# Re-ranking the preparation of mixed rows and tying late ScalarE operations to the newest cast

## The chip, the cores and the metric

The kernel runs on one core of a Trainium2 chip. The metric is device time in microseconds (us) of one execution; several executions give a median. A profile was taken of one further execution.

## The reference, cut to what matters

One layer of a streaming encoder is computed for 2048 new frames (the prompt) and 8 short streams of 16 frames (the sample), all of width 1024, in float32:

```python
h = rmsnorm(x, g_mix_pre)
y, new_k, new_v, new_conv = parallel_mixer(h, ...)   # banded attention | depthwise conv, then @ w_out
x = x + rmsnorm(y, g_mix_post)
h = rmsnorm(x, g_mem_pre)
x = x + rmsnorm(memory_attention(h, mk, mv, w_mq, w_mo), g_mem_post)   # 4 heads, 256 memory tokens
h = rmsnorm(x, g_ffn_pre)
f = (silu(h @ w_gate) * (h @ w_up)) @ w_down
x = x + rmsnorm(f, g_ffn_post)
```

The outputs are the rows x of both groups and the updated caches.

## The kernel before, in words

**Arithmetic.** Every float32 product is made of three matmuls of two rounded parts: a value is cast to its high part on ScalarE (`nc.scalar.copy`), the low part is the difference (VectorE or GpSimd), and `mm3` (lines 268 to 270) adds high x high, high x low and low x high; `mm3h` (line 276) does the same for two halves of 512 columns. So ahead of each group of matmuls stands one cast and one subtraction per operand. Large products are built from seven block products instead of eight, with sums and differences of blocks around them.

**Order.** The program is written in Python loops; a scheduler then places each instruction on its engine's queue by rank (the order of tracing, raised by `high_priority(offset=...)`) and by when it expects its inputs. `issue_after(ins)` makes everything traced inside it stand behind the instruction `ins`. An engine runs its queue strictly in order, so an operation that waits holds up whatever stands behind it. Work that may float is kept in Python generators, from which a loop takes one step at a time with `next`.

**Stages.** The trace has them in this order: memory and input projections, banded attention, the mixing of rows (`mixout`, about 842 to 1100 us), the cross stage (`phase_cross`, about 1100 to 1422), gate and up (`gate_up`, about 1422 to 2400), and down.

**mixout** takes 17 tiles of 128 rows, the sample's tile first. For each tile 48 matmuls (line 276) multiply the mixed rows by the resident weight. `ahead(i)` prepares the tile after the next: `by_column` (GpSimd, line 952) lays out softmax weights, `prep` (lines 995 to 1014) loads the convolution's half (line 998), spreads the weights by one matmul (line 1003), multiplies the attention half (VectorE, 1006), casts both halves (ScalarE, 1012) and takes their low parts (VectorE, 1013), and `weigh` (937 to 946) prepares softmax weights of a later tile. Behind a tile follow Squares (1061), a GpSimd reciprocal root (1062, 286, 287), the scaling (VectorE, 1065), the residual and a store. From the third tile on, a generator `fill` (`cross_sample`) is drawn on: the sample's whole cross attention, whose weights are loaded (1114), cast (ScalarE, 1108) and split (VectorE, 1109). Its steps stand behind the newest low part, `last_prep`.

**phase_cross** takes 16 steps, 8 for the scores and 8 for the output, of seven products each in PSUM banks a, b, a, b, c, d, c. While a step multiplies, the generator `aforms` transposes and splits the rows of the next step (PE 1258, ScalarE 1267, VectorE or GpSimd 1268, sums at 1274 to 1292). The evictions (1457 to 1476) collect the blocks in the rows `ya` and `yb`, of which four tiles exist. What remains of a step floats in `tails`: `softmax` (max 1309, exps 1312, store 1317), `rows_out` (Square 1326, gain 1327, root 286/287, residual 1334, store 1335, a second norm by 294 and 1341), `forms_out` (GpSimd subtractions and stores, 1353 to 1362), `natural` (the same forms for rows loaded again: load 1374, Square 1377, root 1379/1380, scaling 1382, then GpSimd), and `combine`. The function `between`, called after each product, takes one step of each tail, behind the newest eviction.

**gate_up** multiplies weight forms (`wforms`: loads 1539, GpSimd sums 1546 to 1549, casts 1551, low parts 1552) by row forms (`tform`: loads 1526, transposes 1529, casts 1531, low parts 1532) and applies silu (copy 1588, Tanh 1595 and 1613, VectorE 1591 to 1616). Two more `natural` generators are left in `todo`; one step of it is taken per weight tile in group 0 from f = 5 on, behind `done`, the last VectorE operation (1616).

Of the kernel before, what the change touches and what calls it, by code (L numbers as in the profile page):

```python
# [8 lines left out]
F32 = mybir.dt.float32  # L9
F32R = mybir.dt.float32r  # L10
BF16 = mybir.dt.bfloat16
AF = mybir.ActivationFunctionType
# [5 lines left out]
P = 128  # L18
# [118 lines left out]
class Build:  # L137
# [842 lines left out]
    def mixout(self, ctx):  # L980
        nc, A = self.nc, self.A
        sbF, sbR = self.sbF, self.sbR
        (ft, fr), ff = self.flex(ctx, (2048, F32), (2048, F32R)), self.fa
        pool = (Region().lay(sbF, 34.5, ("wf", 4, 3), ("gbc", 4, 1))
                .at("fq", 2, (sbF, [4, 6, 8, 10])).at("ct", 2, (ff, [2, 10])).lay(ff, 0, ("an", 2, 1)).at("po", 4, (ff, [5]), (sbF, [0])).at("spo", 4, (ff, [22]))
                .lay(ff, 12, ("junk", 2, 1), ("xt", 4, 2), ("sh", 8, 1), ("ss", 0.03125, 6), ("rstd", 0.03125, 6),
                     ("nmx", 0.03125, 1), ("sm", 0.03125, 1), ("ri", 0.03125, 1)).lay(ff, 26, ("sgain", 4, 1))
                .at("mh", 4, (sbR, [40, 88])).at("ml", 4, (sbR, [44, 92]))
                .lay(sbR, 96, ("sTh", 4, 1), ("sTl", 4, 1)).lay(ft, 0, ("sT", 8, 1))
                .at("kvh", 4, (sbR, [64, 80]), (fr, [0])).at("kvl", 4, (sbR, [104, 84]), (fr, [4])))  # L990
        ps_y = ps_p = ps_so = Region().lay(self.ps, 0, ("y", 2, 4), ("p", 2, 2), ("so", 4, 1))
        for _ in self.wo_load:
            pass
        ws, self.w = self.wo, pool
        gbc = self.gain(pool, "g_mix_post", "gbc")
        def prep(t):
            ct = self.t(pool, [P, 4, P], F32, "ct", 2)
            nc.sync.dma_start(ct[:, :, :].rearrange("p a b -> p (a b)"), self.cs[t])
            if t == S_TILE:
                att = self.attS[:, :, :]  # L1000
            else:
                pt = self.t(ps_p, [P, 512], F32, "p")
                nc.tensor.matmul(pt[:, :], self.spread[:, :, :].rearrange("p o d -> p (o d)"),
                                 self.rj[:, :, :].rearrange("p j q -> p (j q)"), start=True, stop=True)
                an = self.t(pool, [P, 4, P], F32, "an", 1)
                nc.vector.tensor_tensor(an[:, :, :], self.attT[:, t, :, :],
                                        pt[:, :].rearrange("p (j q) -> p j q", q=P), ALU.mult)
                att = an[:, :, :]
            mh = self.t(pool, [P, KC, P], F32R, "mh", 2)
            ml = self.t(pool, [P, KC, P], F32R, "ml", 2)  # L1010
            for sl, src in ((slice(4, 8), ct[:, :, :]), (slice(0, 4), att)):
                nc.scalar.copy(mh[:, sl, :], src)
                self.last_prep = nc.vector.tensor_tensor(ml[:, sl, :], src, mh[:, sl, :].bitcast(F32), ALU.subtract)
            ready[t] = (mh, ml)

        def ahead(i):

            if 0 < i < len(order) - 1:
                self.by_column(order[i + 1])
                yield  # L1020
                prep(order[i + 1])
            yield
            if 0 < i < len(order) - 2:
                yield from self.weigh(order[i + 2], ps_p, "p")

        order = [S_TILE] + list(range(NPT))
        ready = {}
        with self.tc.high_priority(offset=HP2):
            for t in order[:2]:
                prep(t)  # L1030
        fill, due, self.last_tile = iter(()), 0.0, False
        for i, t in enumerate(order):
            mh, ml = ready.pop(t)
            self.last_tile = i >= len(order) - 2
            pre = ahead(i)
            xt = self.t(pool, [P, D], F32, "xt", 2)
            nc.sync.dma_start(xt[:, :], self.rows("x", t))
            if i in range(8, 16, 2):
                sums = self.combine(pool, 0, i // 2 - 4, 1)
            y = [self.t(ps_y, [P, 512], F32, "y")[:, :] for _ in range(2)]  # L1040
            for k in range(KC):
                if i >= 8 and k % 3 == 1:
                    next(sums, None)
                event = self.mm3h(y, mh[:, k, :], ml[:, k, :], ws[k][0], ws[k][1], k == 0, k == KC - 1)
                if k == 1:
                    self.mixed = event
                if k % 2:
                    next(pre, None)
                    due += RATE if i >= FROM else 0.0
                    while due >= 1:  # L1050
                        with self.tc.issue_after(self.last_prep.ins):
                            next(fill, None)
                        due -= 1
            for _ in pre:
                pass
            ss = self.t(pool, [P, 2], F32, "ss")
            junk = self.t(pool, [P, D], BF16, "junk")
            po = self.t(pool, [P, D], F32, "po")
            cols = [slice(o * 512, (o + 1) * 512) for o in range(2)]
            for o in range(2):  # L1060
                nc.scalar.activation(junk[:, cols[o]], y[o], AF.Square, accum_out=ss[:, o:o + 1])
            nc.gpsimd.tensor_tensor(ss[:, 0:1], ss[:, 0:1], ss[:, 1:2], ALU.add)
            r = self.rstd(pool, ss[:, 0:1], 1.0 / D)
            for o in range(2):
                nc.vector.scalar_tensor_tensor(po[:, cols[o]], y[o], r[:, :], gbc[:, cols[o]], ALU.mult, ALU.mult)
            nc.gpsimd.tensor_tensor(po[:, :], po[:, :], xt[:, :], ALU.add)
            nc.gpsimd.dma_start(self.x1[t], po[:, :])
            if i == 0:
                fill, due = self.cross_sample(pool, ps_so, ps_p), 0.0
        self.last_tile = True  # L1070
        for _ in fill:
            pass
# [129 lines left out]
    def phase_cross(self, ctx):  # L1202
# [48 lines left out]
        def aforms(src, out):  # L1251
# [12 lines left out]
            def split(x, engine):  # L1264
                hi = self.t(pool, [P, 4, P], F32R, "ah")
                lo = self.t(pool, [P, 4, P], F32R, "al")
                nc.scalar.copy(hi[:, :, :], x)
                engine.tensor_tensor(lo[:, :, :], x, hi[:, :, :].bitcast(F32), ALU.subtract)  # L1268
                out.append((hi, lo))

            p21, p22 = turn(xb, 0), turn(xb, 1)
# [94 lines left out]
        def natural(g, p):  # L1366
# [2 lines left out]
            xb = self.t(pool, [P, 2, 512], F32, "nb")[:n]  # L1369
            tt = self.t(pool, [P, 2, 512], F32, "nt")[:n]  # L1370
            dst = self.hn[g]
            for x, (t, r0) in zip((xa, xb), PAIRS[g][p][:2]):
                x2 = x.rearrange("p a b -> p (a b)")
                nc.sync.dma_start(x2, self.x2[t][r0:r0 + n, :])
                junk = self.t(pool, [P, D], BF16, "junk", 1)
                ss = self.t(pool, [P, 1], F32, "ss", 6)
                nc.scalar.activation(junk[:n, :], x2, AF.Square, accum_out=ss[:n, :])
                r = self.t(pool, [P, 1], F32, "rstd", 6)
                nc.gpsimd.tensor_scalar(r[:n, :], ss[:n, :], 1.0 / D, EPS, ALU.mult, ALU.add)
                nc.gpsimd.tensor_tensor(r[:n, :], r[:n, :], self.mhalf[:n, 0:1], ALU.pow)  # L1380
                yield
                nc.vector.scalar_tensor_tensor(x2, x2, r[:n, :], gffn[:n, :], ALU.mult, ALU.mult)
                yield
            nc.gpsimd.tensor_tensor(tt[:, 0, :], xb[:, 0, :], xa[:, 0, :], ALU.subtract)
            nc.gpsimd.dma_start(dst[:n, p, 0:2, :], xa)
# [27 lines left out]
        for s in range(2 * n):  # L1413
# [15 lines left out]
            def between(j):  # L1429
                if j >= 0 and s == n - 1:  # L1430
                    nbf.append(bform(f2, j))
                next(gen, None)
                if j == 2 and s + 2 <= last:
                    src[s + 2] = fetch(s + 2)
                if j == 1 and s == 2:
                    tails.append(natural(2, 2))
                if j == 4 and s in (1, 4):
                    tails.append(self.combine(pool, 1, s // 4 * 2, 2))
                for g in list(tails):
                    with self.tc.issue_after(self.evict.ins) if self.evict else ExitStack():  # L1440
                        over = next(g, tails) is not None
                    if over:
                        tails.remove(g)
# [58 lines left out]
    def gate_up(self, ctx):  # L1502
# [63 lines left out]
        for g in range(3):  # L1566
            n = sum(p[2] for p in PAIRS[g])
            for fp in range(NF // 2):
# [4 lines left out]
                for x in range(2):  # L1573
# [36 lines left out]
                    after(6)  # L1610
                    tt(x2, x2, c, ALU.add)
                    th = self.t(pool, [P, 3 * P], F32, "th")[:, :n]
                    nc.scalar.activation(th, x2, AF.Tanh, scale=0.5)
                    stt(th, th, 1.0, x2, ALU.add, ALU.mult)
                    dst = af[:, 3 if x == 0 else 5, :n]
                    done = stt(dst, th, 0.5, x3, ALU.mult, ALU.mult)
# [2 lines left out]
                    if f < NF - 1 or g < 2:  # L1619
                        w = wforms((f + 1) % NF)  # L1620
                    if g == 0 and f > 4:
                        with self.tc.issue_after(done.ins):
                            next(self.todo, None)
                    if turn:
                        for _ in self.todo:
# [241 lines left out]
```

## Time and profile before

| what | value |
|---|---|
| median of 3 runs | 2872.99 us (2871.47 to 2875.62) |
| the profiled execution's own time | 2869.33 us |
| its span | 2867.6 us |
| TensorE busy | 2818.1 us, 98% of the span |
| VectorE, GpSimd, ScalarE busy | 75%, 52%, 49% |
| mean granted TensorE clock | 0.998 |

The profile's names: PE is TensorE's matmul, PEld its weight load, DVE VectorE, ACT ScalarE, POOL GpSimd, SP the queue that issues most DMAs. L1012 is line 1012 of the kernel before. A group of rows such as "x2" is that many instructions in a row. The bracket at a row's end is the engine's idle time before it and what ended that. `psb` names PSUM, `sbf`, `sbr`, `sbx` and `flexb` name regions of SBUF.

### The profile page before, as it was taken

Reading aid. Unit: us, or ns where it says so; the run is one execution under the profiler, and the core shown is the slowest. Engines: PE = TensorE matmul, PEld = TensorE weight load, DVE = VectorE, ACT = ScalarE, POOL = GpSimd, SP = SyncE. Lnnn points to the kernel's source line nnn. Section 1 sums busy time; section 2 is a strip of 40 time slices with the busy share of each in tenths; the row PEclk is TensorE's granted clock in tenths of the full one; section 3 lists DMA queues with packets and bytes.
Section 4 is the critical chain, followed back from the end, with each engine's and each line's share of the span. In section 5 each row is a group of like instructions: output and inputs, shape, how many; then the busy total and the mean of one; then the engine's idle time right before and its main releaser. Section 6 shows DMA issues by size and latency. Waiting matters only on the chain.

```text
span 2867.6 us, 44831 instructions
## 1 busy us (share of the span) xinstructions
PE 2818.1 (98%) x16056; PEld 2549.2 (89%) x16056; DVE 2154.6 (75%) x3172; ACT 1394.7 (49%) x2803; POOL 1492.2 (52%) x1342
## 2 busy tenths in 40 slices
PE   9999999999999999999999999999999999999998
PEld 8999999988887767888789999999999998888786
DVE  6696795889885337678788888887879997555756
ACT  5545364678883237754443434433344444332433
POOL 1268396741124746627756766465647774325413
PEclk9999999999999999999999999999999999999999
DMA  8726253576625968545663435544343436657664
GB/s 292 248 86 201 96 164 124 182 248 217 217 99 184 336 243 288 195 167 214 230 221 132 152 132 180 196 159 152 126 162 137 146 138 227 219 174 228 232 215 150
DMA packets 216258, 538.26 MB, mean 188 GB/s; under 512 B 21049, under 2 KB 92601, under 8 KB 207706
## 3 DMA queue, kind: packets, MB, share of 16 engines
q1 hardware_dynamic: 206946, 485.72, 49.9%
q0 software_dynamic: 9088, 49.68, 4.8%
q8 instruction: 126, 2.06, 0.3%
q14 instruction: 98, 0.80, 0.1%
HBM read 387.47 MB, written 155.94 MB: 190 GB/s over the span
## 4 chain that ended last, share of the span: by engine, by line
PE 74%; POOL 7%; DVE 6%; DMA 5%; issue 5%; ACT 3%; POOLq 0%; DVEq 0%; SPq 0%; ACTq 0%
PE psb L270 20%; PE psb L268 20%; PE psb L269 20%; PE psb L276 6%; DMA sbf<-in_w_down_dram 2%; PE psb L858 2%; POOL flexb L523 2%; PE psb L827 2%; PE psb L845 1%; POOL sbf L1678 1%; DVE sbr L1552 1%; PE psb L1258 1%; PE psb L1529 1%; PE psb L1128 1%; DVE psb L513 0%
## 5 line engine op out<-in xcount | busy, mean ns | idle before, releaser
L268 PE MATMUL psb<-sbr 128*128 128x384 f32 (+3 forms) x2812 | 958.3, 343 | 4.7 <-ACT sbr L1747 1.5
L269 PE MATMUL psb<-sbr 128*128 128x384 f32 (+3 forms) x2644 | 897.8, 340 | 0.4 <-DVE sbr L1682 0.3
L270 PE MATMUL psb<-sbr 128*128 128x512 f32 (+2 forms) x1852 | 654.2, 355 | 1.8 <-DVE sbr L1748 1.7
L268 PEld LDWEIGHTS psb<-sbr 128*128 128x128 f32 x2812 | 528.9, 188 | 39.9 <-ACT sbr L1747 2.3
L269 PEld LDWEIGHTS psb<-sbr 128*128 128x128 f32 x2644 | 498.4, 188 | 27.0 <-DVE sbr L1682 0.9
L270 PE MATMUL psb<-sbr,sbx 128*128 128x384 f32 (+3 forms) x1400 | 457.0, 328 | 4.1 <-DVE sbx L1268 3.5
L1551 ACT CAST sbr<-sbf 128x512 fp32r<-128x512 f32 x360 | 221.8, 620 | 382.2 <-PE psb L269 321.6
L1552 DVE TENSOR_TENSOR sbr<-sbf,sbr 128x512 fp32r<-128x512 f32 x360 | 365.8, 1019 | 49.7 <-ACT sbr L1551 48.7
L270 PEld LDWEIGHTS psb<-sbr 128*128 128x128 f32 x1852 | 347.2, 188 | 36.9 <-DVE sbr L1748 4.7
L270 PEld LDWEIGHTS psb<-sbr,sbx 128*128 128x128 f32 x1400 | 264.5, 189 | 10.9 <-DVE sbx L1268 3.9
L513 DVE SCALAR_TENSOR_TENSOR psb<-sbf,psb 128x768 f32<-128x768 f32 (+1 forms) x290 | 264.3, 911 | 6.3
L1748 DVE TENSOR_TENSOR sbr<-sbf,sbr 128x384 fp32r<-128x384 f32 (+2 forms) x242 | 160.0, 685 | 89.2 <-ACT sbr L1747 88.1
L263 POOL TENSOR_TENSOR sbx<-sbf,sbr 128x1024 fp32r<-128x1024 f32 (+1 forms) x65 | 150.2, 2315 | 102.1 <-ACT sbr L261 93.9
L1678 POOL TENSOR_TENSOR sbf<-sbf 128x512 f32<-128x512 f32 x77 | 106.7, 1390 | 164.5 <-DMA sbf<-in_w_down_dram 162.7
L1747 ACT CAST sbr<-sbf 128x384 fp32r<-128x384 f32 (+2 forms) x242 | 112.0, 482 | 160.1 <-PE psb L269 133.3
L523 POOL TENSOR_TENSOR flexb<-flexb,flexb 128x128 f32<-128x128 f32 (+1 forms) x180 | 171.1, 951 | 20.5 <-ACT flexb L522 11.1
L268 PE MATMUL psb<-sbr,sbx 128*128 128x384 f32 (+2 forms) x440 | 154.6, 352 | 2.0 <-DVE sbf L1327 1.8
L1546 POOL TENSOR_TENSOR sbf<-sbf 128x512 f32<-128x512 f32 x66 | 96.6, 1463 | 105.3 <-DVE sbr L1552 62.8
L261 ACT CAST sbr<-sbf 128x1024 fp32r<-128x1024 f32 x98 | 102.5, 1050 | 99.1 <-PE psb L269 59.2
L269 PE MATMUL psb<-sbr,sbx 128*128 128x384 f32 (+2 forms) x416 | 143.8, 346 | 0.0
L522 ACT ACTIVATE flexb<-sbf 128x128 f32<-128x128 f32 (+1 forms) x180 | 103.9, 586 | 71.2 <-POOL flexb L523 66.2
L269 PE MATMUL psb<-sbx,sbr 128*128 128x512 f32 (+2 forms) x376 | 133.3, 355 | 0.0
(353 smaller groups left out, 6160.2 us busy)
## 6 DMA issues: line engine op xcount, KB each, us to landing
af<-flexb SPq DMA_DIRECT2D x33, 1344.0 KB, 6.3
sbf<-in_w_down_dram SPq DMA_DIRECT2D x154, 256.0 KB, 3.8
sbf<-in_w_gate_dram SPq DMA_DIRECT2D x66, 512.0 KB, 3.7
sbf<-in_w_up_dram SPq DMA_DIRECT2D x66, 512.0 KB, 3.7
sbf<-af SPq DMA_DIRECT2D x85, 384.0 KB, 4.1
sbf<-x SPq DMA_DIRECT2D x53, 512.0 KB, 3.9
sbf<-in_w_in_dram SPq DMA_DIRECT2D x48, 512.0 KB, 4.4
sbr<-ks POOLq DMA_DIRECT2D x16, 1024.0 KB, 8.7
```

Of the source, the lines that this page charges most:

```text
L263: self.lo_engine.tensor_tensor(lo[:, c], wf[:, c], hi[:, c].bitcast(F32), ALU.subtract)
L268: nc.tensor.matmul(ps, lh, rh, start=start, stop=False, **kw)
L269: nc.tensor.matmul(ps, lh, rl, start=False, stop=False, **kw)
L270: nc.tensor.matmul(ps, ll, rh, start=False, stop=stop, **kw)
L276: last = nc.tensor.matmul(y[o], l, r[:, o * 512:(o + 1) * 512], start=start and x == 0, stop=stop and x == 2)
L513: nc.vector.scalar_tensor_tensor(acc if w < CW - 1 else o, src(w), cwt[:, j, w:w + 1], acc, ALU.mult, ALU.add)
L523: nc.gpsimd.tensor_tensor(o, o, v, ALU.add)
L1551: nc.scalar.copy(hs[j][:, :], src[j])
L1552: nc.vector.tensor_tensor(ls[j][:, :], src[j], hs[j][:, :].bitcast(F32), ALU.subtract)
L1678: nc.gpsimd.tensor_tensor(acc[:, :], acc[:, :], q[:, :], ALU.add if s > 0 else ALU.subtract)
L1747: nc.scalar.copy(ch[:, m], a[:, x, m])
L1748: nc.vector.tensor_tensor(cl[:, m], a[:, x, m], ch[:, m].bitcast(F32), ALU.subtract)
```

## The change

No instruction is added or removed; five edits change what stands behind what.

1. In `mixout`, `by_column` and `prep` of the tile ahead are traced at a rank raised by 200.
2. The steps of `fill` stand behind the newest cast of mixed rows (`prep_cast`, ScalarE 1012) as well as behind its low part.
3. `natural` issues both loads in its first step, both Squares and roots in its second, and both scalings in its third and fourth; before, each row's load, Square and root came together.
4. In the cross stage a step of the tails stands behind the newest cast of `aforms` (ScalarE 1267) as well as behind the newest eviction. (`self.low` is kept but used nowhere.)
5. In `gate_up` a step of `todo` stands behind the last Tanh (ScalarE 1613) as well as behind `done`.

```diff
-                nc.scalar.copy(mh[:, sl, :], src)
+                self.prep_cast = nc.scalar.copy(mh[:, sl, :], src)
...
-                self.by_column(order[i + 1])
+                with self.tc.high_priority(offset=HP2):
+                    self.by_column(order[i + 1])
                 yield
-                prep(order[i + 1])
+                with self.tc.high_priority(offset=HP2):
+                    prep(order[i + 1])
...
-                        with self.tc.issue_after(self.last_prep.ins):
+                        with self.tc.issue_after(self.last_prep.ins), self.tc.issue_after(self.prep_cast.ins):
                             next(fill, None)
...
-                nc.scalar.copy(hi[:, :, :], x)
-                engine.tensor_tensor(lo[:, :, :], x, hi[:, :, :].bitcast(F32), ALU.subtract)
+                self.cast = nc.scalar.copy(hi[:, :, :], x)
+                low = engine.tensor_tensor(lo[:, :, :], x, hi[:, :, :].bitcast(F32), ALU.subtract)
+                if engine is nc.vector:
+                    self.low = low
...
-            for x, (t, r0) in zip((xa, xb), PAIRS[g][p][:2]):
-                x2 = x.rearrange("p a b -> p (a b)")
-                nc.sync.dma_start(x2, self.x2[t][r0:r0 + n, :])
+            flat = [x.rearrange("p a b -> p (a b)") for x in (xa, xb)]
+            for x, (t, r0) in zip(flat, PAIRS[g][p][:2]):
+                nc.sync.dma_start(x, self.x2[t][r0:r0 + n, :])
+            yield
+            rs = []
+            for x in flat:
...
+            yield
+            for x, r in zip(flat, rs):
+                nc.vector.scalar_tensor_tensor(x, x, r[:n, :], gffn[:n, :], ALU.mult, ALU.mult)
                 yield
...
-                    with self.tc.issue_after(self.evict.ins) if self.evict else ExitStack():
+                    with (self.tc.issue_after(self.evict.ins) if self.evict else ExitStack(),
+                          self.tc.issue_after(self.cast.ins)):
                         over = next(g, tails) is not None
...
-                    nc.scalar.activation(th, x2, AF.Tanh, scale=0.5)
+                    sig = nc.scalar.activation(th, x2, AF.Tanh, scale=0.5)
...
-                        with self.tc.issue_after(done.ins):
+                        with self.tc.issue_after(done.ins), self.tc.issue_after(sig.ins):
                             next(self.todo, None)
```

In the changed kernel a line's number is up to 9 higher than before; in the rows below 1063 is 1061, 1110 is 1108, 1269/1270 are 1267/1268, 1278/1283/1288/1296 are 1274/1279/1284/1292, 1331 and 1338 are 1327 and 1334, 1345 is 1341, 1384 is 1377, 1469 is 1460, and 1560, 1597, 1604, 1622 are 1551, 1588, 1595, 1613.

ScalarE where the row mixing begins (846 and 862 are the last of the attention, 261 the output weight's casts, 1108 the sample's weight casts, 1012 the casts of mixed rows, 1061 Squares):

```order
-L1108 CAST sbr<-sbf 128x1024
-L846 CAST sbx<-psb 128x512
+L846 CAST sbx<-psb 128x512 x2
 L261 CAST sbr<-sbf 128x1024 x2
 L862 COPY flexb_169<-psb 64x512
 L846 CAST sbx<-psb 128x512 x2
 L1012 CAST sbr<-flexb_169 128x512
-L1061 ACTIVATE flexb_169<-psb 128x512 x2
-L1108 CAST flexb_8205<-sbf 128x1024
+L1063 ACTIVATE flexb_169<-psb 128x512 x2
 L1012 CAST sbx<-flexb_169 128x512 x2
-L1108 CAST sbr<-sbf 128x1024
```

Three weight casts leave this place; they come back behind the next tile's casts.

VectorE in the same place, as it stands after the change (939, 940 and 937 belong to `weigh`, 1067 is 1065):

```order
L1013 TENSOR_TENSOR sbr<-flexb_169,sbr 128x512
L939 CAST sbr<-sbf 128x8
L1013 TENSOR_TENSOR sbx<-flexb_169,sbx 128x512
L940 TENSOR_TENSOR sbr<-sbf,sbr 128x8
L1067 SCALAR_TENSOR_TENSOR flexb_169<-psb,flexb_169,sbf 128x512
L1013 TENSOR_TENSOR sbx<-flexb_169,sbx 128x512
```

Before, both 1013 of `sbx` stood behind 1065; now one of them stands ahead of it.

VectorE in the last step of the cross stage that has rows to split (1268 low parts, 1274 to 1292 sums of blocks, 1460 an eviction, 1327 and 1334 rows leaving, 1341 their second norm), before:

```order
L1268 TENSOR_TENSOR sbx<-psb,sbx 128x512
L1279 TENSOR_TENSOR flexb_9919<-flexb_9919,psb 128x512
L1284 TENSOR_TENSOR flexb_9919<-psb,flexb_9919 128x512
L1460 TENSOR_TENSOR sbf<-sbf,psb 128x512
L1268 TENSOR_TENSOR flexb_9923<-psb,flexb_9923 128x512
L1327 TENSOR_TENSOR sbf<-sbf 128x512
L1292 TENSOR_TENSOR flexb_9919<-psb,flexb_9919 128x512
L1341 SCALAR_TENSOR_TENSOR sbf<-sbf,flexb_9895 128x1024
L1334 SCALAR_TENSOR_TENSOR sbf<-sbf 128x1024
L1327 TENSOR_TENSOR sbf<-psb,sbf 128x512
```

And after:

```order
L1270 TENSOR_TENSOR sbx<-psb,sbx 128x512
L1278 TENSOR_TENSOR flexb_9919<-psb,flexb_9919 128x512
L1331 TENSOR_TENSOR sbf<-sbf 128x512
L1283 TENSOR_TENSOR flexb_9919<-flexb_9919,psb 128x512
L1288 TENSOR_TENSOR flexb_9919<-psb,flexb_9919 128x512
L1469 TENSOR_TENSOR sbf<-sbf,psb 128x512
L1338 SCALAR_TENSOR_TENSOR sbf<-sbf 128x1024
L1270 TENSOR_TENSOR flexb_9923<-psb,flexb_9923 128x512
L1296 TENSOR_TENSOR flexb_9919<-psb,flexb_9919 128x512
L1345 SCALAR_TENSOR_TENSOR sbf<-sbf,flexb_9895 128x1024
L1331 TENSOR_TENSOR sbf<-psb,sbf 128x512
```

The residual sum 1334 has moved ahead of 1268, 1292 and 1341, and 1327 of the half rows ahead of two of the sums.

ScalarE in gate_up where the first `natural` of `todo` has its Squares (1551 weight casts, 1588, 1595 and 1613 the silu), before:

```order
L1588 COPY sbf<-psb 128x384
L1551 CAST sbx<-sbf 128x512
L1551 CAST sbr<-sbf 128x512
L1377 ACTIVATE sbf<-sbf 128x1024 x2
L1551 CAST sbr<-sbf 128x512
L1613 ACTIVATE flexb_12539<-flexb_12539 128x384
L1551 CAST sbr<-sbf 128x512
L1595 ACTIVATE flexb_12539<-psb 128x384
```

And after, several weight tiles further on:

```order
L1622 ACTIVATE flexb_12539<-flexb_12539 128x384
L1384 ACTIVATE sbf<-sbf 128x1024
L1560 CAST sbr<-sbf 128x512
L1384 ACTIVATE sbf<-sbf 128x1024
L1560 CAST sbr<-sbf 128x512
L1604 ACTIVATE flexb_12539<-psb 128x384
```

The two Squares were one behind the other ahead of a Tanh; they now stand behind a Tanh, with a weight cast between them.

More of the change, by code (lines that the diff above doesn't have):

```diff
@@ L1371, in natural @@
             dst = self.hn[g]
-            for x, (t, r0) in zip((xa, xb), PAIRS[g][p][:2]):
-                x2 = x.rearrange("p a b -> p (a b)")
-                nc.sync.dma_start(x2, self.x2[t][r0:r0 + n, :])
+            flat = [x.rearrange("p a b -> p (a b)") for x in (xa, xb)]
[4 more added lines that the diff above has]
+            for x in flat:
                 junk = self.t(pool, [P, D], BF16, "junk", 1)
                 ss = self.t(pool, [P, 1], F32, "ss", 6)
[L1377 to L1382, printed above, removed]
+                nc.scalar.activation(junk[:n, :], x, AF.Square, accum_out=ss[:n, :])
+                rs.append(self.t(pool, [P, 1], F32, "rstd", 6))
+                nc.gpsimd.tensor_scalar(rs[-1][:n, :], ss[:n, :], 1.0 / D, EPS, ALU.mult, ALU.add)
+                nc.gpsimd.tensor_tensor(rs[-1][:n, :], rs[-1][:n, :], self.mhalf[:n, 0:1], ALU.pow)
+            yield
+            for x, r in zip(flat, rs):
+                nc.vector.scalar_tensor_tensor(x, x, r[:n, :], gffn[:n, :], ALU.mult, ALU.mult)
                 yield
```

## The prediction

> **What bounds the kernel now.** I read the busy shares first, then TensorE's busy time by stretches, then the waits of TensorE stretch by stretch, and last the rows around each wait. The busy shares, engine by engine (busy us, share of the span, instructions):
>
> ```profile
> PE 2818.1 (98%) x16056; PEld 2549.2 (89%) x16056; DVE 2154.6 (75%) x3172; ACT 1394.7 (49%) x2803; POOL 1492.2 (52%) x1342
> ```
>
> TensorE is the bound: whatever the change does on the other engines can only move the 2% in which TensorE stands still. Where those are in the part that the change touches is told by TensorE's stretches (length, busy, instructions, granted clock, DMA share, GB/s):
>
> ```profile
> 840.00:870.00 30.00, 27.32 (x150) 1.00 0.46 149
> 1100.00:1130.00 30.00, 24.62 (x110) 0.94 0.84 314
> 1130.00:1420.00 290.00, 287.78 (x1378) 1.00 0.59 205
> 1420.00:1500.00 80.00, 72.95 (x401) 1.00 0.64 219
> ```
>
> Idle are 2.7 us at the start of the row mixing, 5.4 at the start of the cross stage, only 2.2 in the 290 us of its steady part, and 7.1 around the start of gate_up. Each has its releaser in TensorE's waits (total us, times, longest), taken in four stretches from 840 to 1760:
>
> ```profile
> PE psb L276 <- ACT sbx L1012: 1.4, 1, 1.4
> PE psb L276 <- DVE flexb L1109: 0.9, 1, 0.9
> PE psb L276 <- DVE sbr L263: 0.5, 1, 0.5
> PE psb L276 <- DVE sbx L1013: 0.4, 1, 0.4
> ...
> PE psb L270 <- DVE sbx L1268: 3.5, 1, 3.5
> PE psb L268 <- ACT sbf L1457: 1.3, 2, 1.1
> ...
> PE psb L1529 <- DVE sbr L1532: 1.8, 2, 1.2
> PE psb L268 <- DVE sbf L1327: 1.8, 1, 1.8
> PE psb L268 <- DVE flexb L1602: 1.5, 2, 1.4
> ...
> PE psb L268 <- DVE flexb L1602: 0.7, 1, 0.7
> ```
>
> The change adds no instruction and takes none away; it can gain what these rows hold and lose whatever new waits it makes. The largest, 3.5 us behind L1268, stands where the order of all engines is unchanged, so I leave it in; the 1.8 behind L1532 too, where the casts and loads of gate_up's first forms hardly move.
>
> **Part 1, row mixing (the raised rank and the second anchor).** The first three tiles' rows on ScalarE, TensorE and VectorE (start, us, engine, line, operation, count, idle before and who ended it):
>
> ```profile
> 855.87 1.05 ACT L1108 CAST sbr<-sbf 128x1024 fp32r<-128x1024 f32 x1
> 856.82 0.58 ACT L846 CAST sbx<-psb 128x512 fp32r<-128x512 f32 x1
> 864.54 1.04 ACT L1108 CAST flexb<-sbf 128x1024 fp32r<-128x1024 f32 x1
> 865.48 1.14 ACT L1012 CAST sbx<-flexb 128x512 fp32r<-128x512 f32 x2
> ...
> 859.66 1.66 PE L276 MATMUL psb<-sbr 128*128 128x512 f32 x6 [0.53 <-DVE sbr L263]
> 866.67 1.20 PE L276 MATMUL psb<-sbr,sbx 128*128 128x512 f32 x4 [1.36 <-ACT sbx L1012]
> 868.25 2.11 PE L276 MATMUL psb<-sbr,sbx 128*128 128x512 f32 x8 [0.39 <-DVE sbx L1013]
> ...
> 866.92 1.28 DVE L1013 TENSOR_TENSOR sbx<-flexb,sbx 128x512 fp32r<-128x512 f32 x2
> ```
>
> Three L1108 casts of the next stage's weights (1.05 each) leave these places. The one at 855.87 stood ahead of the casts that feed L263; without it TensorE's 0.53 goes. The one at 864.54 stood ahead of the two L1012 casts: they come about 1 us earlier, so the 1.36 shrinks, but the next matmuls wait for both low halves of L1013, and of these the first now passes ahead of L1065 while the second still stands behind it. The low halves are done one operation of 0.64 us (half of the 1.28) earlier, and that, not the 1.36, is what this stall can give; the wait is otherwise handed on from 866.67 to 868.25. I take 0.5 + 0.4 = **0.9 us**. The displaced weight casts are what may be late next: their matmuls are those that already wait 0.9 us on L1109. I leave that row as it is. Bounds: a loss of 0.9 (nothing gained, that row doubled) and a gain of 2.3, all of the rows behind L1012, L263 and L1013.
>
> **Part 2, the tails of the cross stage behind the newest cast.** In the steady part TensorE idles 2.2 us in 290, so there is little to win, and I put it at 0. What a tail waits for is a cast, and a cast waits for TensorE to free a slot, so tails now walk in TensorE's pace. The softmax's first exps free PSUM bank a; they get one cast (0.6) later, where the next use of the bank is four products away. What can become late is the store of the rows that free a y tile: see the slower rival.
>
> The piece that I count is the last mixed step:
>
> ```profile
> 1416.65 0.68 DVE L1268 TENSOR_TENSOR sbx<-psb,sbx 128x512 fp32r<-128x512 f32 x1
> 1417.25 0.68 DVE L1279 TENSOR_TENSOR flexb<-flexb,psb 128x512 f32<-128x512 f32 x1
> ...
> 1419.64 1.81 DVE L1327 TENSOR_TENSOR sbf<-sbf 128x512 f32<-128x512 f32 x1
> 1421.98 1.27 DVE L1341 SCALAR_TENSOR_TENSOR sbf<-sbf,flexb 128x1024 f32<-128x1024 f32 x1
> 1423.17 2.30 DVE L1334 SCALAR_TENSOR_TENSOR sbf<-sbf 128x1024 f32<-128x1024 f32 x1
> 1427.48 0.69 DVE L1327 TENSOR_TENSOR sbf<-psb,sbf 128x512 f32<-128x512 f32 x1 [2.00 <-ACT sbf L1326]
> ...
> 1425.57 1.06 ACT L294 ACTIVATE sbf<-sbf 128x1024 bf16<-128x1024 f32 x1 [2.28 <-DVE sbf L1334]
> 1426.76 0.60 ACT L1326 ACTIVATE sbf<-psb 128x512 bf16<-128x512 f32 x1
> ...
> 1422.85 3.79 POOL L1268 TENSOR_TENSOR flexb<-flexb,flexb 128x512 fp32r<-128x512 f32 x2 [1.93 <-ACT flexb L1267]
> ```
>
> Bank a is free when L1326 and L1327 have read it (1427.48 + 0.69 = 1428.2), and both stood behind L294, which waited for L1334. In the new order L1334 stands ahead of L1268, L1292 and L1341 instead of behind them. Worked forward: L1268 starts at 1416.65; a 512-wide operation follows the one before it by 0.60 (1417.25 less 1416.65). L1268, L1274, L1279, L1284 and L1460 at 0.60 each and L1327 at 1.75 bring L1334 to 1421.4. It ends at 1422.7 if it is as short as L1341 (1.3 by its row at 1421.98), at 1423.7 with its own 2.30. L1268, L1292 and L1341 (0.6 + 0.6 + 1.3) and L1327 then end at 1425.8 or 1426.8, ScalarE's casts lying beside them. TensorE came for the bank at about 1426.4 (1428.2 less 1.8). So the wait of 1.8 goes, or 0.4 of it stays. The 2.30 is the row nearest in kind, with GpSimd's L1268 beside it, so I take **1.4 us**; bounds 0 and 1.8 (what it could lose is the slower rival's).
>
> [...]
>
> **Part 3, gate_up (loads ahead of the Squares, todo behind Tanh).**
>
> ```profile
> 1488.14 1.06 ACT L1377 ACTIVATE sbf<-sbf 128x1024 bf16<-128x1024 f32 x1 [2.49 <-DMA sbf<-x]
> 1627.77 1.06 ACT L1377 ACTIVATE sbf<-sbf 128x1024 bf16<-128x1024 f32 x1 [3.21 <-DMA sbf<-x]
> ...
> 1491.02 0.69 DVE L1552 TENSOR_TENSOR sbr<-sbf,sbr 128x512 fp32r<-128x512 f32 x1 [2.87 <-ACT sbr L1551]
> ```
>
> At 1488 both Squares stood in ScalarE's queue before their rows had landed; the casts L1551 behind them made VectorE idle 2.87 us, and L1602 kept TensorE 1.4 us a little later. Now the loads are a step ahead and the Squares several weight tiles later, with a cast between the two. Two Squares of 1.06 without the wait cost what the second pair shows: at 1627.77 even a wait of 3.21 went by with a single wait of TensorE, 0.7 us, in the whole stretch from 1500 to 1760, so VectorE's lead there hides such a pause and nothing is late next. I take **1.4 us**; bounds 0 and 1.5. The 0.7 I let stand, since its row names no moved instruction.
>
> **Sum.** 0.9 + 1.4 + 1.4 = 3.7 us. The profiled execution took 2869.33 us, its span 2867.6; it would become 2865.6. It lies 3.7 under the median of the runs, 2872.99 (2871.47 to 2875.62), so from the median the forecast is **2869.3 us**, 0.13% less.
>
> **The rivals.** *Given back.* TensorE comes earlier to gate_up, but its first forms (waits on L1532, 1.8 us, and the rows' stores before them) are ready no sooner, and the second wait of the row mixing is set by L1013. For it: VectorE is the busiest helper there, and the wait rows name it. Against: L1334, on that chain, is moved forward itself. Then only the 1.4 of part 3, or nothing, is left: 2871.6 to 2873.0; I name it at 2872.3.
>
> *More than counted.* The rest of the rows goes too: mixing 1.4 more, L1109 0.9, L1457 1.3, 0.4 at the last step, and the 0.7: 4.7 more, together 8.4, so 2864.6. For it: ScalarE's queue held each of them at some point. Against: five separate repairs, three of which I could not follow to the releaser.
>
> *Slower: the y tiles come free later.* There are four y tiles, so the eviction L1457 of a step writes into one that the step two before must have stored:
>
> ```profile
> 1373.27 0.59 ACT L1457 COPY sbf<-psb 128x512 f32<-128x512 f32 x1 [6.07 <-DMA hn<-sbf]
> 1373.90 0.50 PE L268 MATMUL psb<-sbr,flexb 128*128 128x512 f32 x1 [1.08 <-ACT sbf L1457]
> ...
> ACT sbf L1457 <- DMA hn<-sbf: 15.2, 5, 6.1
> ```
>
> ScalarE waits for that store in five steps already, and in one of them TensorE has waited 1.08 us for it. A tail that has to stand behind one more cast makes its store later. It decides from the point at which the store lands after the next product has ended, and then costs TensorE as long as it is late. If all 14 steps that reuse a tile were as late as this one: 14 x 1.08 = 15.1, less the 3.7: 2872.99 + 11.4 = 2884.4. Against it: GpSimd's rank of the stores' subtractions is hardly changed, and in four of the five steps TensorE lost next to nothing.
>
> *The clock.* In the unchanged piece TensorE idled 3.48 us at once and then ran at a granted clock of 0.57 for 4 us (a row of TensorE's timeline, and a stretch with its length, the busy time of PE, PEld, DVE, ACT and POOL, granted clock, DMA share, GB/s):
>
> ```profile
> 1107.05 0.50 PE L270 MATMUL psb<-sbr,sbx 128*128 128x512 f32 x1 [3.48 <-DVE sbx L1268]
> ...
> 1108.00:1112.00 4.00, 3.75 (x11) 2.44 (x10) 4.00 (x5) 2.02 (x3) 1.94 (x2) 0.57 1.02 412
> ```
>
> That cost 0.43 x 4 = 1.7 us. If the idle time were cut or fell otherwise, the time would be 2869.3 - 1.7 = 2867.6; nothing in the new order does that.
>
> [...]
>
> **How the numbers follow.** Forecast (2867.3 to 2871) 0.33; given back 0.17; more than counted 0.25; slower 0.21; the clock 0.04, all within the bounds of the first. What a measurement of this kernel can tell from no change is about 0.2%, 5.7 us: under 2867.3 is faster, over 2878.7 slower. Faster has "more than counted" and some of the forecast's and the clock's edge: 0.30. Slower has most of its rival (some of it ends between 2873 and 2878): 0.19. The rest, 0.51, is the same. The range runs from 2861 (8.4, the clock's 1.7, and 2 of the runs' spread) to 2881 (11 of the slower rival's 14 steps: 11 x 1.08 less 3.7 is 8.2), and leaves out the rest of that rival.
>
> **What would show it.** Right: no wait of TensorE on L1327 at the end of the cross stage (or 0.4), none on L1602 soon after gate_up's start, ScalarE's Squares of natural with no wait for a load, the waits on L1268 (3.5) and L1532 unchanged, and less than 2.3 in all behind L1012, L263 and L1013. Wrong: waits of TensorE on L1457 in many steps, with longer idle time of ScalarE on the stores of hn or zs; a new wait on the weight casts of the sample's stage (L1108, L1109); or a gate_up start that idles longer than 7.1 us.

## The result and the profile after

The changed kernel takes 2879.08 us (median of 13 runs, 2877.28 to 2885.18) beside 2873.54 for the kernel before (13 runs on the same chip): ratio 1.0023, 95% interval [1.0016, 1.003]. By the ratio it is slower by 6.6 us; the medians lie 5.5 apart. (Two experiments below have one far longer execution among their 11, 3087.45 and 15516.17 us, which their ratios leave out.) The forecast was 2869.3; the range to 2881 holds the time, the chance given to "slower" was 0.19. The profiled execution took 2878.41 us, its span is 2876.6 (before 2867.6), its mean granted clock 0.995 (before 0.998).

In the changed kernel 1269/1270 are 1267/1268 of before (casts and low parts), 1249 is 1247 (`fetch` scales a row by its root), 1260 is 1258 (transposes), 1466, 1475 and 1485 are 1457, 1466 and 1476 (evictions), 1063 is 1061, 1538/1541 are 1529/1532, 1611 is 1602. Other variants shift by a few lines more or less.

TensorE's waits after, in three stretches from 840 to 1510:

```profile
PE psb L276 <- DVE sbx L1013: 0.5, 1, 0.5
PE psb L276 <- DVE sbr L1013: 0.4, 1, 0.4
PE psb L276 <- ACT sbx L1012: 0.4, 1, 0.4
...
PE psb L270 <- DVE sbx L1270: 3.3, 1, 3.3
PE psb L1260 <- DVE sbx L1270: 2.9, 1, 2.9
PE psb L270 <- POOL flexb L1270: 2.0, 1, 2.0
...
PE psb L1538 <- DVE sbr L1541: 3.6, 2, 2.4
PE psb L1538 <- DMA sbf<-hn: 1.5, 2, 0.8
PE psb L268 <- DVE flexb L1611: 0.5, 1, 0.5
```

The rows that the change was to shorten are shorter: L1012 1.4 to 0.4, L1109 and L1327 gone at their places, L1602 (now L1611) 1.5 to 0.5. Two long waits have come into the cross stage, 2.9 us, and 2.0 us where 0.7 stood before, beside shorter ones of up to 1.0; at gate_up's start L1541 has 3.6 instead of 1.8.

The stages can be timed by three ScalarE lines whose first and last start the trace gives: the Squares of the row mixing, the first eviction of each cross step, the first silu copy of gate_up (line, instructions, duration in ns, first and last start). Before:

```profile
L1061 ACT ACTIVATE flexb<-psb x34: 582/590/602, 863.4 to 1101.6; 128x512 bf16<-128x512 f32 x34
L1457 ACT COPY sbf<-psb x16: 563/586/589, 1110.6 to 1439.1; 128x512 f32<-128x512 f32 x16
L1588 ACT COPY sbf<-psb x66: 417/473/479, 1460.1 to 2388.9; 128x384 f32<-128x384 f32 x44, 128x320 f32<-128x320 f32 x22
```

After:

```profile
L1063 ACT ACTIVATE flexb<-psb x34: 575/588/597, 861.6 to 1097.0; 128x512 bf16<-128x512 f32 x34
L1466 ACT COPY sbf<-psb x16: 567/587/590, 1106.9 to 1443.9; 128x512 f32<-128x512 f32 x16
L1597 ACT COPY sbf<-psb x66: 416/472/478, 1470.0 to 2396.2; 128x384 f32<-128x384 f32 x44, 128x320 f32<-128x320 f32 x22
```

Row mixing took 238.2 us and takes 235.4: **2.8 gained**. The cross stage took 328.5 and takes 337.0: **8.5 lost**. From its last first-eviction to gate_up's first copy it was 21.0 and is 26.1: **5.1 lost**. Within gate_up 928.8 became 926.2: 2.6 gained. Between the last Square and the first eviction it was 9.0 and is 9.9. The 1.8 us less ahead of the row mixing and the 1.7 more behind gate_up stand nearly all where no order changed, and are put down to the difference of two executions.

Idle time and clock share the loss. These rows are TensorE's in the cross stage and from there to gate_up's first copy (stretch, length, TensorE busy, matmuls, granted clock, DMA share, GB/s), before and then after:

```profile
1110.60:1439.10 328.50, 323.32 (x1538) 1.00 0.60 207
1439.10:1460.10 21.00, 19.43 (x110) 1.00 0.83 285
...
1106.90:1443.90 337.00, 326.80 (x1538) 0.99 0.58 200
1443.90:1470.00 26.10, 21.01 (x108) 0.92 0.70 226
```

In the two together TensorE stood idle for 6.8 us and stands idle for 15.3: 8.5 more. It was busy for 342.7 us and is busy for 347.8, with two matmuls fewer: 5.1 more, at a lower granted clock. Over the whole span idle time grew by 4.9 us and busy time by 4.1 (2818.1 to 2822.2, with 16056 matmuls in both).

**What happens in the cross stage.** ScalarE and GpSimd around one step, before (start, us, engine, line, operation, idle before and its releaser; L294 and L1247 are the two halves of `fetch`'s norm of two rows that are needed two steps later, L286 and L287, a reciprocal root on GpSimd, stand between them; L977 are `combine`'s four subtractions, the last two of them here):

```profile
1203.00 1.06 ACT L294 ACTIVATE sbf<-sbf 128x1024 bf16<-128x1024 f32 x1 [1.70 <-DMA sbf<-x]
1204.19 1.06 ACT L294 ACTIVATE sbf<-sbf 128x1024 bf16<-128x1024 f32 x1
...
1205.25 0.57 ACT L1267 CAST flexb<-psb 128x512 fp32r<-128x512 f32 x1
1205.71 0.62 ACT L1267 CAST flexb<-flexb 128x512 fp32r<-128x512 f32 x1
1206.49 1.15 ACT L1247 ACTIVATE sbf<-sbf 128x1024 f32<-128x1024 f32 x1 [0.16 <-POOL sbf L287]
...
1208.53 1.14 ACT L1247 ACTIVATE sbf<-sbf 128x1024 f32<-128x1024 f32 x1
1209.57 0.61 ACT L1267 CAST flexb<-flexb 128x512 fp32r<-128x512 f32 x1
...
1210.99 0.57 ACT L1267 CAST sbx<-psb 128x512 fp32r<-128x512 f32 x1
...
1199.80 4.89 POOL L977 TENSOR_TENSOR sbf<-sbf 128x1024 f32<-128x1024 f32 x2
...
1205.91 0.55 POOL L287 TENSOR_TENSOR sbf<-sbf,mhalf 128x1 f32<-128x1 f32 x1
```

And after, with what GpSimd, VectorE and TensorE do there, and ahead of it an earlier place:

```profile
1123.32 2.05 POOL L287 TENSOR_TENSOR sbf<-sbf,mhalf 128x1 f32<-128x1 f32 x2
1125.34 1.97 POOL L1270 TENSOR_TENSOR flexb<-flexb,flexb 128x512 fp32r<-128x512 f32 x1
...
1127.37 0.50 PE L270 MATMUL psb<-flexb,flexb 128*128 128x512 f32 x1 [2.03 <-POOL flexb L1270]
...
1202.02 1.05 ACT L294 ACTIVATE sbf<-sbf 128x1024 bf16<-128x1024 f32 x1
...
1208.18 1.15 ACT L1249 ACTIVATE sbf<-sbf 128x1024 f32<-128x1024 f32 x1 [4.06 <-POOL sbf L287]
...
1211.24 1.06 ACT L294 ACTIVATE sbf<-sbf 128x1024 bf16<-128x1024 f32 x1 [0.42 <-DMA sbf<-x]
...
1213.99 1.15 ACT L1249 ACTIVATE sbf<-sbf 128x1024 f32<-128x1024 f32 x1 [1.09 <-POOL sbf L287]
1215.05 0.60 ACT L1269 CAST flexb<-flexb 128x512 fp32r<-128x512 f32 x1
1215.56 0.57 ACT L1269 CAST sbx<-psb 128x512 fp32r<-128x512 f32 x1
...
1203.99 0.18 POOL L286 TENSOR_SCALAR sbf<-sbf 128x1 f32<-128x1 f32 x1
1204.25 2.40 POOL L977 TENSOR_TENSOR sbf<-sbf 128x1024 f32<-128x1024 f32 x1
1206.62 1.53 POOL L287 TENSOR_TENSOR sbf<-sbf,mhalf 128x1 f32<-128x1 f32 x1
...
1216.22 0.69 DVE L1270 TENSOR_TENSOR sbx<-psb,sbx 128x512 fp32r<-128x512 f32 x1 [2.34 <-issue]
...
1216.97 1.12 PE L1260 MATMUL psb<-ident,sbf 128*128 128x128 f32 x4 [2.89 <-DVE sbx L1270]
```

Before, GpSimd had done all four subtractions when it came to the roots, and on ScalarE the second row's Square and two casts stood between the halves of the first norm. So the half that waits for GpSimd came when GpSimd was nearly done: it waited 0.16 us. After, the last subtraction (2.40 us) stands between the two operations of the first root. `combine` is one of the tails that edit 4 holds back; `fetch` is not held. ScalarE stands for 4.06 us before the first norm. The second row's Square now stands behind that norm, so its root is late too, and the second norm waits 1.09 us more, ahead of two casts; the cast of `sbx` comes at 1215.56, its low part at 1216.22, and TensorE, which stands for it, has idled 2.89 us.

The stall at 1127 us, in the first rows, is like it: the low part L1270 on GpSimd stands behind a subtraction and two roots there, where the kernel before has a subtraction and one root. A wait of ScalarE for these roots is not costly by itself: the kernel before has one of 4.20 us at 1118.64, with no wait of TensorE over 0.4 us in the next 10 us. At 1213.99 the casts behind it were needed at once.

### The profile page after: what moved, and what is told of

It reads as the page before. It is cut to its first block, busy times and chain, and to the rows that moved or that the text cites. A ratio compares the mean times of both kernels' runs of the same rounds, so it can differ in the third digit from the quotient of the medians.

```text
span 2876.6 us, 44851 instructions
## 1 busy us (share of the span) xinstructions
PE 2822.2 (98%) x16056; PEld 2553.2 (89%) x16056; DVE 2162.8 (75%) x3172; ACT 1393.1 (48%) x2803; POOL 1492.0 (52%) x1342
## 5 line engine op out<-in xcount | busy, mean ns | idle before, releaser
L263 POOL TENSOR_TENSOR sbx<-sbf,sbr 128x1024 fp32r<-128x1024 f32 (+1 forms) x65 | 149.9, 2310 | 106.0 <-ACT sbr L261 94.3
```

The costliest lines, as they stand in the source:

```text
L263: self.lo_engine.tensor_tensor(lo[:, c], wf[:, c], hi[:, c].bitcast(F32), ALU.subtract)
```

## The experiments

My theory is that edit 4 loses by the new order of the cross stage's queues: what is not held comes ahead of what is. The letters of the theories in the expectations hold for their own group of runs and are explained there. "Ratio" is to the kernel before on the same chip, with its 95% interval.

### Which edit loses

Edits 1 and 2 alone (row mixing):

> Edits 1 and 2 alone (raised rank of the preparation, fill behind the newest cast), on the kernel before. Theory A (the gain of the change lies in the row mixing, its loss in the cross stage and behind it): the cross stage starts about 3.4 us earlier, as in the changed kernel (ScalarE's Squares of the last mixed tile: -4.6 there, -1.3 before the change begins), its waits are those of before, so the time is 2870, 3.4 under before. [...]

Measured: 2868.68 us (11 runs), ratio 0.9983 [0.9974, 0.9992], 4.9 us faster. Its Squares span 235.5 us, 2.7 less than before, and its waits behind L1012 and L1013 are those of the changed kernel. The row mixing gains in full.

Edit 4 alone (tails behind the newest cast):

```diff
-                    with self.tc.issue_after(self.evict.ins) if self.evict else ExitStack():
+                    with (self.tc.issue_after(self.evict.ins) if self.evict else ExitStack(),
+                          self.tc.issue_after(self.cast.ins)):
```

> Edit 4 alone (the tails of the cross stage behind the newest cast), on the kernel before. Theory A: this edit carries the whole loss: waits of TensorE of 2 to 3 us near 1125 and 1214, a start of gate_up that waits for its w_up load, and a half-clock window behind each; 9 to 12 us slower than before. Theory B (the loss comes from the mixing edits or from their meeting with this one): within 3 us of before.

Measured: 2882.59 us (6 runs), ratio 1.0030 [1.0019, 1.0042], 8.6 us slower. Edit 4 alone loses no less than the whole change. Its cross stage runs from 1111.8 to 1443.4, 331.6 us, 3.1 more than before; most of its loss stands at gate_up's start, 5.7 us. The stall of 2.0 us is there (2.4), that of 2.9 us is not.

Edits 3 and 5 alone (gate_up):

> Edits 3 and 5 alone (natural's loads ahead of its Squares, todo behind the Tanh), on the kernel before. The prediction's part 3: TensorE's wait on L1602 of 1.4 us at about 1495 goes, 1.4 us faster, all else the same. Rival: it goes, but natural in the cross stage moves too and adds waits there; 0 to 3 us slower.

Measured: 2871.48 us (11 runs), ratio 0.9990 [0.9981, 0.9999]. TensorE's wait for the silu (L1602 of before, here 1606) between 1425 and 1510 went from 1.5 us to this row:

```profile
PE psb L268 <- DVE flexb L1606: 0.2, 1, 0.2
```

All edits but the fourth:

> The change without edit 4. Theory A: the gains of the mixing (3.4) and of gate_up (1.4) without the loss: 4 to 5 us faster than before, about 2868.5, and faster than either kernel. [...] If edit 4 is not the cause of the loss: 2876 or more.

Measured: 2868.83 us (11 runs), ratio 0.9980 [0.9971, 0.9988]. Without edit 4 the change gains 5.7 us; with it, it loses 6.6.

### What in the fourth edit

`fetch` too stands behind the newest cast, so that the norms can't slip ahead of `combine`'s subtractions and the casts:

```diff
+                    with self.tc.issue_after(self.cast.ins):
-                    src[s + 2] = fetch(s + 2)
+                        src[s + 2] = fetch(s + 2)
```

> The changed kernel, with the fetching of the rows two steps ahead (load, Square, root, scaling) held behind the newest cast as well. Theory A (the exps leave ScalarE's queue, and the fetch's scaling, which waits for GpSimd's roots behind the 2.4 us subtractions of combine, takes their place ahead of the casts): the waits of TensorE near 1125 (2.0) and 1214 (2.9) go with the half-clock windows behind them, so 4 to 7 us faster than the changed kernel, 2872 to 2875; the start of gate_up stays as late as in it. Theory B (the exps themselves come late and keep PSUM banks): no gain, 2878 to 2881.

Measured: 2875.57 us (11 runs), ratio 1.0010 [1.0001, 1.0019]. The stall of 2.9 us is gone, and of that of 2.0 us 0.6 is left, as much as in the kernel before (0.7). All four subtractions stand ahead of the roots again. ScalarE's waits for the root between 1095 and 1300 us (total, times, longest) are about those of before (5.7). This row is of the changed kernel, the one under it of this one:

```profile
ACT sbf L1249 <- POOL sbf L287: 10.1, 5, 4.1
```

```profile
ACT sbf L1249 <- POOL sbf L287: 5.9, 3, 3.7
...
L1465 ACT COPY sbf<-psb x16: 562/586/589, 1110.5 to 1441.2; 128x512 f32<-128x512 f32 x16
```

By its evictions (the last row) the cross stage takes 330.7 us instead of 337.0. So the norms' place is shown to be the cause of most of the cross stage's loss: one anchor on `fetch` gives 6.3 of 8.5 us back, 3.3 of it idle time. Whether freeing `combine` instead would do the same was not run. The kernel as a whole gets back 0.13%, about 3.7 us, and the two intervals still touch, since gate_up still starts late: 26.5 us after the last eviction.

The next five runs put edit 4 in force in some steps only, by a condition on the step:

```diff
-                          self.tc.issue_after(self.cast.ins)):
+                          self.tc.issue_after(self.cast.ins) if s < 13 else ExitStack()):
```

Steps 0 to 12:

> The changed kernel, with edit 4 in force for steps 0 to 12 of the cross stage only; in steps 13 to 15 a tail stands behind the newest eviction alone, as before. Theory A: edit 4 loses in two places that have nothing to do with each other, in the first steps (GpSimd's queue, the stalls on sbx and flexb) and at the start of gate_up (the rows' last forms and stores behind the last casts). Then the stalls near 1125 and 1214 us stay and gate_up starts as without edit 4: about 4 us less than the changed kernel, ratio to before 1.000 to 1.001, and no loss between the last eviction of the cross stage and gate_up's third tile beyond 1 us. Theory B: the late start of gate_up is handed on from the earlier steps (rows that have fallen behind); then this kernel is as slow as the changed one, 1.0023, with a gate_up start that loses 5 us.

Steps 13 to 15:

> The changed kernel, with edit 4 in force for steps 13 to 15 of the cross stage only. Theory A: no stall near 1125 and 1214 us, the cross stage as without edit 4, but gate_up's start loses about 5 us: ratio to before 0.9995 to 1.0005. Theory B: nothing is lost anywhere, 0.998 as without edit 4.

Steps 0 to 12, with `fetch` held as above:

> The changed kernel with the fetch of rows two steps ahead also held behind the newest cast, and edit 4 in force for steps 0 to 12 only. Theory A: both losses go, apart from some 2 us in the first steps that were left when the fetch alone was held: 0.998 to 0.9995. Theory B: as with the fetch alone held, 1.001.

Measured: 2880.95 us (6 runs), ratio 1.0029 [1.0016, 1.0041], for the early steps; 2865.88 (9 runs), **0.9974 [0.9965, 0.9984]**, for the last three; 2873.56 (11 runs), 1.0001 [0.9992, 1.001], with `fetch` held, between the figures of its two theories. The last three steps lose nothing. Theory A, as put for these runs (two losses with nothing in common), is wrong on the second: with edit 4 out of force at the end, gate_up starts late all the same, and with it in force only there, in time. The late start is handed on from the earlier steps.

Which of them is told by the eight score steps (0 to 7) against the eight output steps (8 to 15):

> The changed kernel with edit 4 in force for the eight score steps only (steps 0 to 7). Theory A: all of the loss is made where fetch, softmax and combine meet the casts in the first six steps, as stalls of TensorE on sbx and flexb, and what shows at gate_up's start follows from it: as slow as steps 0 to 12 alone, 1.002 to 1.003. Theory B: the start of gate_up is late through the output steps (rows_out and forms_out held behind casts): the score steps alone then lose about 5 us against 0.998, ratio 0.9995 to 1.0005, and gate_up starts as without edit 4.

> The changed kernel with edit 4 in force for the eight output steps only (steps 8 to 15). Theory A: nothing is lost, 0.997 to 0.998, as with the last three steps alone. Theory B: gate_up's start loses 3 to 5 us, 0.9985 to 0.9995.

Measured: score steps 2887.62 us (6 runs), 1.0039 [1.0025, 1.0053]; output steps 2868.21 (10 runs), 0.9977 [0.9968, 0.9986]. The whole loss is made in the score steps. The cross evictions and the wait on the root, score steps in force:

```profile
L1464 ACT COPY sbf<-psb x16: 567/588/593, 1108.5 to 1445.0; 128x512 f32<-128x512 f32 x16
...
ACT sbf L1249 <- POOL sbf L287: 10.4, 5, 4.0
```

And with the last three steps in force, the evictions and TensorE's longest wait from 1100 to 1425, which stands ahead of the stage's first eviction; the next longest is 1.2:

```profile
L1464 ACT COPY sbf<-psb x16: 563/586/589, 1106.4 to 1433.8; 128x512 f32<-128x512 f32 x16
...
PE psb L270 <- DVE sbx L1270: 3.4, 1, 3.4
```

336.5 us in the one, as in the changed kernel; 327.4 in the other, 1.1 less than before, with no wait on the half rows (L1327 of before) at the stage's end. The kernel with edit 4 in the last three steps has the lowest time of all here, though its interval overlaps those of four others, and beats both kernels: the one before by 7.3 us, the changed one by 1.0023 - 0.9974 = 0.49%, about 14 us.

### Why gate_up starts late, and the clock

In the changed kernel the first load of up-weights waited 7.2 us for the store of an output row in the same memory; the kernel before has a wait of 6.1 us on such a store ahead of a load of gate-weights. So two weight slots were exchanged, in the changed kernel and in the one without edit 4:

```diff
-.at("wf", 4, (sbF, [20, 24, 28, 38.5]))
+.at("wf", 4, (sbF, [20, 28, 24, 38.5]))
```

> The changed kernel with two of the four weight slots of gate_up exchanged, so that the first w_up load takes the place that the earlier of the two last row stores frees. Theory A (that load waits 7.2 us for the later store and makes the start of gate_up wait): it is issued about 8 us sooner, TensorE's waits on L1541 (3.6) and the half-clock window there shrink, 3 to 6 us faster than the changed kernel, 2873 to 2876. Theory B (the start is bound by VectorE or by the rows' forms): the load is early and the waits stay, within 1.5 us of the changed kernel.

> The change without edit 4, with the two weight slots exchanged. The load is 2.4 us sooner at most (it waited 0.2 us for the later store in before), so 0 to 2 us faster than without the exchange, 2867 to 2869. If VectorE bounds the start, no difference.

Measured: 2886.48 us (5 runs), ratio 1.0057 [1.0044, 1.0070], and 2870.86 (11 runs), 0.9999 [0.999, 1.0008]. Both are worse than without the exchange. The wait of 7.2 us is still there, now ahead of a load of gate-weights, and TensorE's stalls at gate_up's start stay. That the late up-weights are the cause is not borne out.

Twelve matmuls that add nothing to the result were put into the first product's 3.5-us pause, in the kernel without edit 4, to keep TensorE from idling there:

```diff
...
+                    for i in range(12):
+                        with self.tc.issue_after(m.ins):
+                            m = mm(warm[0], ah[:, 0, :], bh[:, 0, :], start=True, stop=True, skip_group_check=True)
...
```

> The change without edit 4, with 12 extra matmuls into a PSUM bank that is cleared before its use, placed in the 3.5 us wait of the cross stage's first product; they add no result. Theory A (the idle stretch there halves the clock for about 3.4 us): TensorE works through the wait, the granted clock between 1104 and 1112 stays at 1.00 instead of about 0.8, 1.7 us faster, 2867. Theory B (the clock falls for another reason, such as the transposes ahead of it): the clock row stays and the time is that without them, 2868.8; if the extra matmuls end after the wait, 0.3 to 1 us slower.

Measured: 2874.35 us (11 runs), ratio 1.0004 [0.9995, 1.0013], against 0.9980 without them: about 7 us lost. A matmul of another product now stands in the queue ahead of the twelve and waits for L1067 to have read its bank, so the pause became 6.56 us instead of 3.5:

```profile
1107.03 0.77 PE L268 MATMUL psb<-sbr,flexb 128*128 128x512 f32 x1 [6.56 <-DVE flexb L1067]
```

The pause was not filled, so the run says nothing on the clock; it is inconclusive.

## Why the prediction was wrong

**The step that failed** is in part 2: "In the steady part TensorE idles 2.2 us in 290, so there is little to win, and I put it at 0." Little to win was right. For what could be lost I followed only the operations that the edit holds back ("they get one cast (0.6) later"). I did not ask how they then stand to what is not held: a subtraction of `combine` fell between the operations of a root, and two norms that wait for GpSimd stood ahead of casts that TensorE waits for. The cross stage lost 8.5 us, and gate_up's start 5.1. That TensorE idled little there was no sign that it couldn't idle more: its idle time in the cross stage went from 5.2 us to 10.2.

**The clock** failed with it. The prediction let the clock's loss of 1.7 us only go away, and took it that the change "can only move the 2% in which TensorE stands still". But behind the new stalls of 2.03 and 2.89 us TensorE ran at 0.57 from 1128 to 1132 and at 0.60 from 1216 to 1220, and TensorE's busy time grew too, by 5.1 us in the rows above. How much of the 6.6 us is clock can only be estimated: the granted clock is on record for every execution, with a mean of 0.9959 over the 13 of the changed kernel and of 0.9969 to 0.9971 in four sets of the kernel before (16 to 28 executions each, from the experiments above). A thousandth of the span is 2.9 us, so that is some 3 us, about half; it is a high estimate, as the clock is low in some idle time too (0.50 from 1467 to 1468 in the changed kernel, where TensorE is busy for 0.09 us).

**Part 1** was right in its direction and too small: 0.9 us forecast, 2.8 in the trace's Squares and 4.9, interval 2.3 to 7.5, in the run of these edits alone. The wait was not "handed on" from L1012 to L1013: L1012's fell by 1.0 us, and L1013's rows are 0.5 and 0.4 against 0.4 and 0.4. The wait on L1109 (0.9), which I left in and feared would double, is gone. L263's, of which I counted 0.5, fell only from 0.5 to 0.3.

**The last mixed step** was right: 1.4 us forecast, and the wait of 1.8 on L1327 at 1426 is gone. With edit 4 in the last three steps the cross stage takes 327.4 us; without edit 4 it takes 328.9 by this row, 1.5 more, and has a wait of 1.7 on the half rows:

```profile
L1463 ACT COPY sbf<-psb x16: 562/585/587, 1108.9 to 1437.8; 128x512 f32<-128x512 f32 x16
```

**Part 3** was right: 1.4 us forecast; L1602's wait fell from 1.5 to 0.2 in the run of these edits alone (3.0 us faster, interval 0.3 to 5.5).

**"The 1.8 behind L1532 too ... hardly move"** failed: 3.6, and 1.5 on the loads of hn. The runs show that this comes from the score steps. By which of the scheduler's placements it gets there was not isolated, so the cause of these 5.1 us stays open.

**The rivals.** *Slower* came true in sign but not in mechanism: ScalarE's waits for the stores of hn fell from 18.8 us (6) to 11.6 (3) between 1100 and 1440, and TensorE's wait on that eviction from 1.3 to 0.2. The y tiles played no part. *More than counted* was right for the row mixing only. *Given back* is not what happened: the gains stayed, and something else was lost.

## What to carry to other kernels

Where an operation is held back on an in-order queue, list what now stands ahead of it and what it now stands ahead of, on every engine that it uses, and ask of each whether its input will be there: here one norm that was not ready stopped ScalarE for 4.06 us. Try an anchor by stages: the same line lost 1.0039 - 0.9980 = 0.59%, 17 us, in the score steps against the kernel without it, and nothing in the output steps. Read the clock behind a new stall too: here two stalls were followed by stretches of 4 us at 0.57 and at 0.60, and beside 8.5 us more of idle time stood 5.1 us more of busy time for the same work.

## What the runs showed of the hardware

TensorE's granted clock fell after pauses shorter than the 3.48 us of the kernel before, and not after each long one. In the changed kernel it idled 2.03 us up to 1127 and then ran at 0.57, and 2.89 us up to 1217 and then ran at 0.60 (length, busy times, clock, DMA share, GB/s):

```profile
1128.00:1132.00 4.00, 4.00 (x15) 3.11 (x14) 2.81 (x4) 4.00 (x9) 3.92 (x4) 0.57 0.28 113
1216.00:1220.00 4.00, 3.03 (x9) 2.58 (x10) 3.67 (x5) 2.16 (x7) 2.24 (x2) 0.60 0.98 385
```

In the kernel with edit 4 in the last three steps it idled 3.40 us at the place where the kernel before idled 3.48, and kept its full clock, where the kernel before fell to 0.57:

```profile
1103.41 0.50 PE L270 MATMUL psb<-sbr,sbx 128*128 128x512 f32 x1 [3.40 <-DVE sbx L1270]
...
1104.00:1108.00 4.00, 3.36 (x14) 2.28 (x13) 4.00 (x5) 2.18 (x4) 1.89 (x3) 1.00 1.03 401
1108.00:1112.00 4.00, 4.00 (x20) 3.27 (x19) 4.00 (x4) 2.44 (x5) 3.92 (x2) 1.00 0.79 292
```

In the kernel before the clock was at 0.50 from 1108.4 to 1111.8, for 3.4 us. Why pauses so alike ended differently was not shown.

A tiny operation on GpSimd was long at times: by the trace, whose GpSimd spans are rough, the root L287 on one column takes 0.55 us in most rows, and 1.53 at 1206.62, while a 1024-wide VectorE operation lay beside it (1205.46 to 1207.73); the kernel before has two of 1.54, at 1127.93 and 1138.98. That the one operation made the other long was not shown. ScalarE's 4.06 us hold one of these.
